# Feed-forward transposes placed six chunks behind their products, relu and square in one VectorE instruction, down projection trailing by six chunks

## The chip, the cores and the metric

The kernel runs on one core of a Trainium2 chip. The metric is the device time of one execution in microseconds. A core has five engines that run side by side, each through its own queue in order: PE (TensorE, matrix products and transposes), DVE (VectorE), ACT (ScalarE), POOL (GpSimd) and SP (SyncE, which only issues loads and stores here). Data comes from HBM into SBUF by DMA, and PE writes its results into PSUM banks.

## The reference

One decoder block on 256 tokens of width 2048, in float32. Only the last part is touched by the change.

```python
proj = x @ w_in                      # conv group and gated linear attention follow
...
mix = concatenate([y_conv, y_gla]) @ w_out
x = layer_norm(DN_ALPHA * x + mix, ln1_g, ln1_b)
ff = square(relu(x @ w_ff_up)) @ w_ff_down      # 2048 -> 8192 -> 2048
x = layer_norm(DN_ALPHA * x + ff, ln2_g, ln2_b)
```

## The kernel before

**Split products.** Every float32 factor is written as a sum of two parts in a shorter format, hi and lo. ACT rounds (`copy`, L108) and DVE subtracts (L109); together that is a *split*. PE then does three matmuls for each pair of tiles (L153 to L155: hi by hi, hi by lo, lo by hi). A weight *chunk* is 256 rows by 512 columns, 512 KB, and takes one load, one split and six matmuls for each half of 128 tokens that it serves. Such six matmuls are called one *product* here.

**Buffers.** Raw chunks lie in 13 buffers (`raw`), split chunks in five (`hl`). A load waits until DVE has freed a raw buffer, and a split waits until PE has freed a split buffer.

**The feed-forward part.** The 8192 hidden columns are eight groups g of 1024. Group 0 (`up_first`) is computed plainly. Groups 1 to 7 (`up`) use a scheme of seven products in place of eight for the 2 x 2 blocks of (tokens, columns): 28 steps s, which are seven phases p of four chunks j. The up chunk of a step is called p_j here (`hl_up_2_3` is phase 2, chunk 3). The phases read these raw tiles: 0: r11; 1: r11 + r12 (DVE, L719), then r11 gets more rows by an accumulating DMA from POOL (L728); 2: r21; 3: the accumulated r11, then accumulated once more; 4: r12 + r22 (DVE, L724, the *third sum*); 5: r22; 6: r11. So four buffers hold r11 over the whole group, four hold r12 from phase 1 to phase 4, and five are left for what streams: r21, r22 and the chunks of the down projection.

Phases end with a combination that gives a 128 x 512 block of the group's output: `end_2` (straight from PSUM bank a), `end_7` (v), `end_3` (x12) and `end_4` (u). Each goes through relu and square, and then `put` transposes it on PE (`pt_h`, L216) and splits it into the pair `hT`, which the down projection reads as its left factor.

**Order on PE.** The products are emitted in the order in which PE is to run them. `lag.after(mm)` is called after every product; it counts down the entries of `lag.soon`, and a transpose whose count is over is ordered behind that product. The main loop at the end runs one up step, adds 4/7 to `owed`, and lets a generator emit one down chunk for each whole unit in `owed`. A down chunk serves both halves of the tokens: two products and two calls of `lag.after`. Names like `dn_512_2` are column block 512, chunk 2. When both chunks and tokens of a column block are done, DVE adds the bank to `y` (L802). A scheduler sets the order on the other engines from the order of the program and its own estimates.

Of the kernel before, what the change touches and what calls it, by code (L numbers as in the profile page):

```python
# [12 lines left out]
AF = mybir.ActivationFunctionType  # L13
ALU = mybir.AluOpType
# [45 lines left out]
def hymba_block(ctx, tc, x, x_t, w_in, conv_w, conv_g, w_gate, gate_b, gla_g, w_out,  # L60
                ln1_g, ln1_b, w_up, w_down, ln2_g, ln2_b, out):
    nc = tc.nc
# [188 lines left out]
    with ExitStack() as p1:  # L251
# [225 lines left out]
        def conv_block(j):  # L477
# [26 lines left out]
            def done_b(t, ps):  # L504
# [8 lines left out]
                for g in range(4):  # L513
                    cols = slice(g * P, (g + 1) * P)
                    nc.vector.scalar_tensor_tensor(y[:, cols], y[:, cols], rstd[:, g:g + 1], cg[:, cols],
                                                   op0=ALU.mult, op1=ALU.mult)
                lag0.soon.append([1 + WAIT_C, lambda: put(y, mixT["conv"], j, t, f"c{j}{t}")])

# [29 lines left out]
    with ExitStack() as p2:  # L548
# [99 lines left out]
        def x1lhs(kt, t):  # L648
            return part(x1T, kt, t)

        def hidden(r, hT, i, t, name, wait):

            nc.vector.tensor_mul(r, r, r)
            lag.soon.append([wait, lambda: put(r, hT, i, t, name)])

        def up_first(hT):

            for i in range(GROUP // NB):
                def done(t, ps, i=i):
                    r = ht.tile([P, NB], F32, tag="relu", name=f"relu_0_{i}_{t}")  # L660
                    nc.scalar.activation(r, ps, AF.Relu)
                    hidden(r, hT, i, t, f"h0_{i}_{t}", 1 + WAIT_H)
                if i == 1:
                    homes[:] = [[(hlp, "hl")], 0]
                    lag.lag = 0
                project(lag, w_up, list(range(KT)), i * NB, NB, x1lhs, done, f"up0_{i}",
                        lags=LAGS if i == 0 else None, before=sums_ahead if i == 1 else None)
# [37 lines left out]
        def up(g, hT):  # L705
# [27 lines left out]
            banks, kept = {}, {}  # L733

            def out(x, i, t, where=None):
                r = x if where is None else where
                nc.scalar.activation(r, x, AF.Relu)
                hidden(r, hT, i, t, f"h{g}_{i}_{t}", 2)

            def end_1():  # L740
                kept["p1"] = tmp("p1")
# [40 lines left out]
            for s, (p, j) in enumerate(steps):  # L782
                _, lhs, bank, then, end = plan[p]
                prepare(s + 1)
                name = f"up{g}_{p}_{j}"
# [78 lines left out]
        downs = iter(())  # L864

        def all_downs():
            for g in range(NG - 1):
                yield from down(g, hTs[g])

        downs, owed = all_downs(), -1.5  # L870
        for g in range(1, NG):
            hTs.append(t8_pair(f"hT_{g}"))
            for _ in up(g, hTs[g]):
# [63 lines left out]
```

## Time and profile before

| | |
|---|---|
| median of 3 runs (lowest to highest) | 1116.71 us (1114.16 to 1119.34) |
| profiled execution: time, span | 1116.4 us, 1114.7 us |
| granted TensorE clock, mean | 0.988 |
| DVE, ACT, POOL busy | 837.2, 598.9, 63.9 us |
| HBM traffic | 222 GB/s over the span |
| up step 1 of group 1 begins, products of group 7 end | about 440, 1048 us |

The span runs from the first to the last instruction. Busy times say how long an engine worked, and the waits say for whom it stood still. An engine that is not the bound may wait at no cost. In rows of a timeline the columns are start, duration, engine, line, operation, tiles and shape, and in brackets the idle time before and who ended it.

### The profile page before, as it was taken

What the parts mean: (1) busy time and instruction counts of PE and PEld (TensorE: products, weight loads), DVE (VectorE), ACT (ScalarE), POOL (GpSimd) and SP (SyncE); (2) the same over time, 40 slices, a digit from 0 to 9 for tenths busy, and PEclk for the clock granted to TensorE, in tenths of its full rate; (3) what the DMA queues carried; (4) which work ended last, traced back from release to release, by engine and by line L of the source; (5) the groups of instructions that cost most, each with busy time, mean ns of one, the idle gap of its engine ahead of it and who ended that gap; (6) DMA issues with size and microseconds to landing.
All of it is one profiled execution on the core that took longest, in us unless ns stands there. A gap on an engine that the chain in (4) does not pass through costs nothing.

```text
span 1114.7 us, 13469 instructions
## 1 busy us (share of the span) xinstructions
PE 1071.6 (96%) x4914; PEld 896.2 (80%) x4914; DVE 837.2 (75%) x958; ACT 598.9 (54%) x695; POOL 63.9 (6%) x74
## 2 busy tenths in 40 slices
PE   9999999999999899999999999999989999989994
PEld 8998888888888778788878877877878877878884
DVE  6555558477655879689789789789879978968867
ACT  6476544436633545556546556556556655645531
POOL 0000000000000110100110110110110110010001
PEclk9999999999999999999999999999999999999998
DMA  9876267676766542997887888788698688688821
GB/s 337 306 254 206 83 209 256 206 225 216 263 225 194 164 159 107 252 258 244 242 228 267 226 228 285 201 239 296 165 252 297 168 251 300 174 232 273 278 63 75
DMA packets 76743, 248.06 MB, mean 223 GB/s; under 512 B 8003, under 2 KB 18259, under 8 KB 76422
## 3 DMA queue, kind: packets, MB, share of 16 engines
q1 hardware_dynamic: 65024, 207.78, 54.7%
q0 software_dynamic: 8064, 29.36, 14.5%
q10 hardware_dynamic: 3590, 10.08, 2.5%
q8 instruction: 38, 0.62, 0.2%
q14 instruction: 27, 0.22, 0.1%
HBM read 244.03 MB, written 3.15 MB: 222 GB/s over the span
## 4 chain that ended last, share of the span: by engine, by line
PE 68%; DVE 14%; DMA 12%; issue 4%; ACT 2%; SPq 0%; DVEq 0%; ACTq 0%
DMA raw_dn<-in_w_ff_down_dram 6%; PE ps_dn L154 6%; PE ps_dn L153 6%; PE ps_dn L155 6%; DMA raw_r<-in_w_ff_up_dram 5%; DVE hl_up L109 5%; DVE hl_dn L109 3%; PE ps_p L155 3%; PE ps_p L153 3%; PE ps_p L154 3%; PE ps_o L155 2%; PE ps_o L154 2%; PE ps_o L153 2%; PE ps_upd L154 2%; PE ps_upd L153 2%
## 5 line engine op out<-in xcount | busy, mean ns | idle before, releaser
L108 ACT CAST hl_up<-raw_r 128x1024 fp32r<-128x1024 f32 x196 | 205.6, 1052 | 107.6 <-PE ps_dn L155 51.5
L109 DVE TENSOR_TENSOR hl_up<-raw_r,hl_up 128x1024 fp32r<-128x1024 f32 x196 | 237.4, 1219 | 30.9 <-ACT hl_up L108 28.4
L108 ACT CAST hl_dn<-raw_dn 128x1024 fp32r<-128x1024 f32 x128 | 134.8, 1053 | 142.8 <-PE ps_dn L155 77.1
L109 DVE TENSOR_TENSOR hl_dn<-raw_dn,hl_dn 128x1024 fp32r<-128x1024 f32 x128 | 156.1, 1220 | 54.4 <-ACT hl_dn L108 53.1
L154 PE MATMUL ps_dn<-hl_dn,hT_hi 128*128 128x512 f32 x496 | 193.5, 390 | 0.5 <-DVE hl_dn L109 0.5
L153 PE MATMUL ps_dn<-hl_dn,hT_hi 128*128 128x512 f32 x496 | 193.3, 390 | 0.0
L155 PE MATMUL ps_dn<-hl_dn,hT_lo 128*128 128x512 f32 x496 | 193.1, 389 | 0.0
L154 PEld LDWEIGHTS ps_dn<-hl_dn,hT_hi 128*128 128x128 f32 x496 | 93.1, 188 | 20.8 <-DVE hl_dn L109 1.3
L153 PEld LDWEIGHTS ps_dn<-hl_dn,hT_hi 128*128 128x128 f32 x496 | 93.1, 188 | 19.8
L155 PEld LDWEIGHTS ps_dn<-hl_dn,hT_lo 128*128 128x128 f32 x496 | 93.1, 188 | 19.4
L728 POOL DMA_DIRECT2D raw_r<-in_w_ff_up_dram x56 | 48.5, 866 | 561.7 <-DVE hl_up L109 530.0
L109 DVE TENSOR_TENSOR hl_p<-raw_p,hl_p 128x824 fp32r<-128x824 f32 (+1 forms) x40 | 40.3, 1016 | 33.4 <-ACT hl_p L108 31.7
L109 DVE TENSOR_TENSOR hl_o<-raw_o,hl_o 128x1024 fp32r<-128x1024 f32 x32 | 38.8, 1222 | 32.9 <-ACT hl_o L108 32.5
L108 ACT CAST hl_o<-raw_o 128x1024 fp32r<-128x1024 f32 x32 | 33.4, 1056 | 45.2 <-PE ps_o L155 31.7
L153 PE MATMUL ps_p<-hl_p,xT_hi 128*128 128x412 f32 (+1 forms) x160 | 56.2, 351 | 0.2 <-ACT xT_hi L108 0.2
L154 PE MATMUL ps_p<-hl_p,xT_hi 128*128 128x412 f32 (+1 forms) x160 | 56.2, 351 | 0.0
L155 PE MATMUL ps_p<-hl_p,xT_lo 128*128 128x412 f32 (+1 forms) x160 | 55.8, 349 | 0.3
L724 DVE TENSOR_TENSOR raw_r<-raw_r,raw_r 128x1024 f32<-128x1024 f32 x28 | 34.2, 1222 | 28.0 <-DMA raw_r<-in_w_ff_up_dram 28.0
L108 ACT CAST hl_p<-raw_p 128x824 fp32r<-128x824 f32 (+1 forms) x40 | 35.1, 885 | 27.1 <-PE ps_p L155 21.4
L154 PE MATMUL ps_upa<-hl_up,x1T_hi 128*128 128x512 f32 x112 | 44.1, 394 | 0.0
L153 PE MATMUL ps_upc<-hl_up,sum_s 128*128 128x512 f32 x112 | 44.1, 394 | 0.0
L153 PE MATMUL ps_upa<-hl_up,x1T_hi 128*128 128x512 f32 x112 | 43.7, 391 | 0.0
(281 smaller groups left out, 2168.2 us busy)
## 6 DMA issues: line engine op xcount, KB each, us to landing
raw_dn<-in_w_ff_down_dram SPq DMA_DIRECT2D x128, 512.0 KB, 5.0
raw_r<-in_w_ff_up_dram SPq DMA_DIRECT2D x112, 512.0 KB, 5.3
raw_r<-in_w_ff_up_dram POOLq DMA_DIRECT2D x56, 512.0 KB, 8.1
raw_o<-in_w_out_dram SPq DMA_DIRECT2D x32, 512.0 KB, 3.5
raw_p<-in_w_in_dram SPq DMA_DIRECT2D x24, 412.0 KB, 5.7
raw_c<-in_w_in_dram SPq DMA_DIRECT2D x16, 512.0 KB, 3.7
raw_u<-in_w_in_dram SPq DMA_DIRECT2D x16, 512.0 KB, 4.3
raw_b<-in_w_in_dram SPq DMA_DIRECT2D x16, 512.0 KB, 4.2
```

The lines of the kernel that those rows point to most:

```text
L108: queued("act", lambda: nc.scalar.copy(hi, src))
L109: queued("dve", lambda: nc.vector.tensor_sub(lo, src, hi.bitcast(F32)))
L153: nc.tensor.matmul(ps[:, :ncol], ah, whi[:, j, cols], start=f, stop=False, skip_group_check=more)
L154: nc.tensor.matmul(ps[:, :ncol], ah, wlo[:, j, cols], start=False, stop=False, skip_group_check=more)
L155: nc.tensor.matmul(ps[:, :ncol], al, whi[:, j, cols], start=False, stop=e, skip_group_check=more)
L724: nc.vector.tensor_add(r12[j], r12[j], r22[j])
L728: return lambda j: nc.gpsimd.dma_start(r11[j], piece(w_up, KH + KC * j, at, NB), accum_op=ALU.add)
```

## The change

Three things change, all in the feed-forward part. The transpose of each output block in groups 1 to 7 stands six calls of `lag.after` behind its product, not two. Blocks that lie in SBUF (v, x12, u) go through relu and square in one DVE instruction, max(x, 0) * x; blocks that come from PSUM (group 0 and `end_2`) get two ACT instructions, relu and then square. The down projection starts 6 chunks behind the up steps, not 1.5.

```diff
+WAIT_UP = 6
+BEHIND = 6
...
-        def hidden(r, hT, i, t, name, wait):
-
-            nc.vector.tensor_mul(r, r, r)
+        def hidden(r, x, hT, i, t, name, wait):
+
+            if r is x:
+                nc.vector.scalar_tensor_tensor(r, x, 0.0, x, op0=ALU.max, op1=ALU.mult)
+            else:
+                nc.scalar.activation(r, x, AF.Relu)
+                nc.scalar.activation(r, r, AF.Square)
             lag.soon.append([wait, lambda: put(r, hT, i, t, name)])
...
                     r = ht.tile([P, NB], F32, tag="relu", name=f"relu_0_{i}_{t}")
-                    nc.scalar.activation(r, ps, AF.Relu)
-                    hidden(r, hT, i, t, f"h0_{i}_{t}", 1 + WAIT_H)
+                    hidden(r, ps, hT, i, t, f"h0_{i}_{t}", 1 + WAIT_H)
...
             def out(x, i, t, where=None):
-                r = x if where is None else where
-                nc.scalar.activation(r, x, AF.Relu)
-                hidden(r, hT, i, t, f"h{g}_{i}_{t}", 2)
+                hidden(x if where is None else where, x, hT, i, t, f"h{g}_{i}_{t}", WAIT_UP)
...
-        downs, owed = all_downs(), -1.5
+        downs, owed = all_downs(), -BEHIND
```

The first place to look at is PE in group 2, around the transpose of the block of `end_2`, whose bank `ps_upa` is done with chunk 2_3. Before (each product is cut to its last matmul):

```order
L155 MATMUL ps_upa_4156<-hl_up_2_3_4392,x1T_lo 128x512
...
L155 MATMUL ps_dn_512_0_4409<-hl_dn_512_0_4406,hT_lo 128x512
...
L155 MATMUL ps_dn_512_1_4416<-hl_dn_512_0_4406,hT_lo 128x512
L216 MATMUL pt_h_0_0_4423<-ident,relu_4401 128x128 x4
L153 MATMUL ps_upb_4434<-hl_up_3_0_4430,sum_q 128x512
```

With the change:

```order
L157 MATMUL ps_upa_4057<-hl_up_2_3_4317,x1T_lo 128x512
...
L157 MATMUL ps_upb_4333<-hl_up_3_0_4329,sum_q 128x512
...
L157 MATMUL ps_dn_0_1_4352<-hl_dn_0_0_4342,hT_lo 128x512
...
L157 MATMUL ps_upb_4333<-hl_up_3_1_4359,sum_q 128x512
...
L157 MATMUL ps_upb_4333<-hl_up_3_2_4369,sum_q 128x512
...
L157 MATMUL ps_dn_0_0_4345<-hl_dn_0_2_4381,hT_lo 128x512
L218 MATMUL pt_h_0_0_4390<-ident,relu_4326 128x128 x4
```

Two products lay between bank and transpose; now six do. Beside phase 3 stands the first column block of the down projection, where the second stood.

The second place is DVE in the same group, from the split of up 2_3 to the split behind the last third sum. Before:

```order
L109 TENSOR_TENSOR hl_dn1_512_0_4406<-raw_dn1_512_0_4404,hl_dn1_512_0_4406 128x1024
L724 TENSOR_TENSOR raw_r12_2_0_4221<-raw_r12_2_0_4221,raw_r22_2_0_4495 128x1024
...
L109 TENSOR_TENSOR hl_dn1_512_2_4453<-raw_dn1_512_2_4451,hl_dn1_512_2_4453 128x1024
L653 TENSOR_TENSOR relu_2_4401<-relu_2_4401 128x512
L109 TENSOR_TENSOR hl_up2_3_2_4468<-raw_r11_2_2_4180,hl_up2_3_2_4468 128x1024
L724 TENSOR_TENSOR raw_r12_2_1_4235<-raw_r12_2_1_4235,raw_r22_2_1_4512 128x1024
L109 TENSOR_TENSOR hl_dn1_512_4_4480<-raw_dn1_512_4_4478,hl_dn1_512_4_4480 128x1024
...
L109 TENSOR_TENSOR hl_up2_4_0_4515<-raw_r12_2_0_4221,hl_up2_4_0_4515 128x1024
L724 TENSOR_TENSOR raw_r12_2_2_4268<-raw_r12_2_2_4268,raw_r22_2_2_4544 128x1024
L724 TENSOR_TENSOR raw_r12_2_3_4281<-raw_r12_2_3_4281,raw_r22_2_3_4556 128x1024
L109 TENSOR_TENSOR hl_dn1_512_6_4527<-raw_dn1_512_6_4525,hl_dn1_512_6_4527 128x1024
```

With the change:

```order
L729 TENSOR_TENSOR raw_r12_2_0_4127<-raw_r12_2_0_4127,raw_r22_2_0_4403 128x1024
L111 TENSOR_TENSOR hl_up2_3_0_4329<-raw_r11_2_0_4050,hl_up2_3_0_4329 128x1024
L111 TENSOR_TENSOR hl_dn1_0_0_4342<-raw_dn1_0_0_4340,hl_dn1_0_0_4342 128x1024
L729 TENSOR_TENSOR raw_r12_2_1_4160<-raw_r12_2_1_4160,raw_r22_2_1_4437 128x1024
...
L111 TENSOR_TENSOR hl_up2_3_2_4369<-raw_r11_2_2_4081,hl_up2_3_2_4369 128x1024
L729 TENSOR_TENSOR raw_r12_2_2_4174<-raw_r12_2_2_4174,raw_r22_2_2_4450 128x1024
L111 TENSOR_TENSOR hl_dn1_0_2_4381<-raw_dn1_0_2_4379,hl_dn1_0_2_4381 128x1024
...
L111 TENSOR_TENSOR hl_up2_4_1_4453<-raw_r12_2_1_4160,hl_up2_4_1_4453 128x1024
L111 TENSOR_TENSOR hT_2_lo_4049<-pt_h2_0_0_4390,hT_2_hi_4048 128x4x128
L729 TENSOR_TENSOR raw_r12_2_3_4206<-raw_r12_2_3_4206,raw_r22_2_3_4481 128x1024
L111 TENSOR_TENSOR hl_dn1_0_6_4464<-raw_dn1_0_6_4462,hl_dn1_0_6_4464 128x1024
```

The square (L653) is gone from between them, and the second and third of the four third sums stand earlier against the chunks of phase 3, the fourth behind the split of `hT`.

The third place is SP's queue where group 1 opens. Before:

```order
L112 DMA raw_r12_1_1_3594<-in_w_ff_up_dram 128x1024
L112 DMA raw_dn0_0_0_3608<-in_w_ff_down_dram 128x1024
L112 DMA raw_r12_1_2_3627<-in_w_ff_up_dram 128x1024
L112 DMA raw_r12_1_3_3640<-in_w_ff_up_dram 128x1024
L112 DMA raw_dn0_0_2_3653<-in_w_ff_down_dram 128x1024
L112 DMA raw_r21_1_0_3670<-in_w_ff_up_dram 128x1024
L112 DMA raw_dn0_0_4_3682<-in_w_ff_down_dram 128x1024
```

With the change:

```order
L114 DMA raw_r12_1_1_3594<-in_w_ff_up_dram 128x1024
L114 DMA raw_r12_1_2_3608<-in_w_ff_up_dram 128x1024
...
L114 DMA raw_r21_1_3_3668<-in_w_ff_up_dram 128x1024
L114 DMA raw_dn0_0_0_3702<-in_w_ff_down_dram 128x1024
L114 DMA raw_dn0_0_2_3741<-in_w_ff_down_dram 128x1024
L114 DMA raw_r22_1_0_3765<-in_w_ff_up_dram 128x1024
L114 DMA raw_dn0_0_4_3782<-in_w_ff_down_dram 128x1024
```

The first down chunk's load stands behind all loads of r12 and r21, and r22_0 follows two loads later. POOL's order is the same in both. From group 2 on, SP's mix of up and down loads is as dense as before, with the down chunks 4.5 later.

## Prediction

> **What bounds the kernel now.** I read the page first, then the list of waits, then the timelines of PE, DVE, ACT and SP around the longest PE waits of the feed-forward part. These are the page's span and busy times:
>
> ```profile
> span 1114.7 us, 13469 instructions
> PE 1071.6 (96%) x4914; PEld 896.2 (80%) x4914; DVE 837.2 (75%) x958; ACT 598.9 (54%) x695; POOL 63.9 (6%) x74
> ```
>
> From the list of waits (us in total, times, longest):
>
> ```profile
> PE pt_h L216 <- DVE relu L653: 17.7, 7, 3.8
> PE pt_h L216 <- DVE v L653: 2.3, 4, 0.7
> DVE raw_r L724 <- DMA raw_r<-in_w_ff_up_dram: 28.0, 17, 3.0
> SPq L112 <- DVE hl_dn L109: 367.1, 118, 15.9
> PE ps_dn L154 <- DVE hl_dn L109: 0.5, 2, 0.3
> ```
>
> PE is the bound: it is idle for 1114.7 - 1071.6 = 43 us in all. 17.7 + 2.3 = 20.0 us of that stand before the feed-forward transposes, which wait for the square (L653) in DVE's queue. Nothing else in the feed-forward part makes PE wait for long yet: the next candidate, a product that waits for DVE's half of a split, costs 0.5 us. But the third and fourth rows say what stands behind: DVE itself waits for r22 (L724), and SP can issue loads only as DVE frees raw buffers.
>
> A wait also costs something after it. These are PE's rows at the five transposes that matter most: the transposes, then the first matmul of the next down chunk, twelve up matmuls later.
>
> ```profile
> 473.87 1.09 PE L216 MATMUL pt_h<-ident,relu 128*128 128x128 f32 x4 [2.57 <-DVE relu L653]
> 478.43 0.39 PE L153 MATMUL ps_dn<-hl_dn,hT_hi 128*128 128x512 f32 x1
> ...
> 561.95 1.03 PE L216 MATMUL pt_h<-ident,relu 128*128 128x128 f32 x4 [2.46 <-DVE relu L653]
> 566.78 0.40 PE L153 MATMUL ps_dn<-hl_dn,hT_hi 128*128 128x512 f32 x1
> ...
> 823.68 0.63 PE L216 MATMUL pt_h<-ident,relu 128*128 128x128 f32 x4 [3.07 <-DVE relu L653]
> 828.50 0.40 PE L153 MATMUL ps_dn<-hl_dn,hT_hi 128*128 128x512 f32 x1
> ...
> 911.40 0.63 PE L216 MATMUL pt_h<-ident,relu 128*128 128x128 f32 x4 [2.33 <-DVE relu L653]
> 914.64 0.39 PE L153 MATMUL ps_dn<-hl_dn,hT_hi 128*128 128x512 f32 x1
> ...
> 1000.36 1.09 PE L216 MATMUL pt_h<-ident,relu 128*128 128x128 f32 x4 [3.82 <-DVE relu L653]
> 1006.10 0.39 PE L153 MATMUL ps_dn<-hl_dn,hT_hi 128*128 128x512 f32 x1
> ```
>
> The same work takes 3.24 us after the wait of 2.33 and 4.56, 4.83, 4.82, 5.74 us after waits of 2.57, 2.46, 3.07, 3.82: PE runs slow for a while after waits of about 2.4 us and more. That is 1.32 + 1.59 + 1.58 + 2.50 = 7.0 us. All that the change could win at the transposes is 20.0 + 7.0 = 27.0 us, 3.9 per group of the seven.
>
> The Trainium skill (TensorE: Matmul & The Clock Gate, Part 1) says that PE's clock falls back after at least one idle window of about 3.4 us. By that only the wait of 3.82 would be slowed, and the win would be at most 22.5 us; the rows show a loss from 2.46 us on, so the trace decides. The sum does not use the page.
>
> **The chain behind the wait.** Rows of the first planned group (g=1): the split of up 2_2 and its product; r22_0's issue, the first third sum; the split of dn 512_4, the issue of r22_3 that follows it, the last third sum, the split of dn 512_6 and its product.
>
> ```profile
> 460.92 1.22 DVE L109 TENSOR_TENSOR hl_up<-raw_r,hl_up 128x1024 fp32r<-128x1024 f32 x1
> 465.70 0.39 PE L153 MATMUL ps_upa<-hl_up,x1T_hi 128*128 128x512 f32 x1
> 467.06 0.39 PE L153 MATMUL ps_upa<-hl_up,x1T_hi 128*128 128x512 f32 x1
> 462.17 0.33 SPq L112 DMA_DIRECT2D raw_r<-in_w_ff_up_dram  x1
> 467.30 1.23 DVE L724 TENSOR_TENSOR raw_r<-raw_r,raw_r 128x1024 f32<-128x1024 f32 x1 [1.30 <-DMA raw_r<-in_w_ff_up_dram]
> 475.92 1.22 DVE L109 TENSOR_TENSOR hl_dn<-raw_dn,hl_dn 128x1024 fp32r<-128x1024 f32 x1
> 477.16 0.33 SPq L112 DMA_DIRECT2D raw_r<-in_w_ff_up_dram  x1
> 484.24 1.23 DVE L724 TENSOR_TENSOR raw_r<-raw_r,raw_r 128x1024 f32<-128x1024 f32 x1 [2.16 <-DMA raw_r<-in_w_ff_up_dram]
> 485.38 1.22 DVE L109 TENSOR_TENSOR hl_dn<-raw_dn,hl_dn 128x1024 fp32r<-128x1024 f32 x1
> 488.18 0.39 PE L154 MATMUL ps_dn<-hl_dn,hT_hi 128*128 128x512 f32 x1
> ```
>
> DVE ends split 2_2 at T = 462.14; SP issues r22_0 at once into the buffer so freed, and it lands 5.1 us later. Nine DVE instructions after that sum, the split of dn 512_4 ends at 477.14 and frees the buffer for r22_3, which lands 7.1 us later. Then the third sum and the split of dn 512_6 end at 486.6 = T + 24.5. PE's product starts at 488.18, only 1.6 us later, although PE had just lost 2.57 + 1.32 = 3.9 us at the transposes. Without that loss PE would come at 484.3 and wait 2.3 us. So part of the old wait is a cover for this chain. PE's step is 467.06 - 465.70 = 1.36 us for an up chunk, twice that for a down chunk.
>
> How early split 2_2 ends before its product (call it s) is 465.92 - 462.14 = 3.8 us here (465.92 is its second matmul, 465.70 + 0.22, the first that reads what DVE writes), and differs between groups; two others, the best and the worst:
>
> ```profile
> 635.11 1.22 DVE L109 TENSOR_TENSOR hl_up<-raw_r,hl_up 128x1024 fp32r<-128x1024 f32 x1
> 641.99 0.39 PE L154 MATMUL ps_upa<-hl_up,x1T_hi 128*128 128x512 f32 x1
> ...
> 987.64 1.22 DVE L109 TENSOR_TENSOR hl_up<-raw_r,hl_up 128x1024 fp32r<-128x1024 f32 x1
> 991.16 0.39 PE L154 MATMUL ps_upa<-hl_up,x1T_hi 128*128 128x512 f32 x1
> ```
>
> That is 5.7 and 2.3 us; I take s = 4.0, the middle of the two ends.
>
> **The change, part by part.** The rows that price it: the square on DVE, the same shape as a scalar_tensor_tensor from SBUF, a Square on ACT; then an accumulating load's time to landing in 446 to 470 us, the first one of group 1, and the first matmul of group 1.
>
> ```profile
> L653 DVE TENSOR_TENSOR relu<-relu 128x512 f32<-128x512 f32 x11 | 7.5, 683 | 0.0
> L693 DVE SCALAR_TENSOR_TENSOR sum_s<-y,y x2: 683/685/687, 402.0 to 424.7; 128x512 f32<-128x512 f32 x2
> L508 ACT ACTIVATE csq<-c 128x512 f32<-128x512 f32 x4 | 2.5, 624 | 3.1 <-DVE c L506 3.1
> raw_r<-in_w_ff_up_dram POOLq DMA_DIRECT2D x3, 512.0 KB, 9.7
> 443.85 1.01 POOL L728 DMA_DIRECT2D raw_r<-in_w_ff_up_dram  x1 [46.39 <-DVE hl_up L109]
> 440.28 0.39 PE L153 MATMUL ps_upa<-hl_up,x1T_hi 128*128 128x512 f32 x1
> ```
>
> Relu and square: 21 outputs (v, x12, u in seven groups) lose a Relu on ACT, and DVE's square becomes one scalar_tensor_tensor of the same 0.68 us. The other 11 (4 of group 0, 7 of end_2) lose DVE's 0.68 us and gain a Square of 0.62 us on ACT. DVE does 7.5 us less over the run, ACT 21 - 11 = 10 instructions less. Nothing of it is on PE's path once the transposes stand later, so its own term is 0, bounded by 0.6 us per group either way.
>
> Transposes: pt_h for end_2 stood two products (2.7 us) behind its bank; now up 3_0, dn 0_0, up 3_1, 3_2 and half of dn 0_2 lie between, 8.2 us. Relu and Square need 1.2 us and stand on ACT. The longest old wait, 3.82, is under the 5.4 us that are added, so these waits go: -27.0 us (bounds -20.0, if PE slows for other reasons, and -27.0).
>
> Down chunks six behind, in groups 2 to 7. PE's work and DVE's are the same in number, but what lies between split 2_2 and the last third sum changes. On PE from 2_2 on: eight up chunks, four down chunks and a transpose (0.37): 8 x 1.36 + 4 x 2.72 + 0.37 = 22.1 us (before 7 x 1.36 + 3 x 2.72 + 0.37 = 18.1). On DVE: r22_0 lands at T + 5.1; third sum 0, splits 3_0 and dn 0_0 end at T + 8.5 (1.14 from start to start: 485.38 - 484.24); that frees r22_2's buffer. Let a load take L. Third sum 2, dn 0_2, 3_3 and dn 0_4 follow, 4 x 1.14: T + 13.1 + L; this frees r22_3's buffer; it lands after L, and third sum 3 and split dn 0_6 take 2.4: T + 15.5 + 2L. PE then waits 15.5 + 2L - 22.1 - s = 2L - 6.6 - 4.0. For L the rows give 5.1 and 7.1; I take the middle, 6.1, as one accumulating load stands before r22_2 and more before r22_3. The wait is 1.6, say 1.5 us, under the length that slows PE. Six groups: +9.0 us. With L = 5.1 it is 0; with 7.1 it is 3.6 and some 2 of slowing, 34 us in all.
>
> Group 1 opens with 13 up chunks alone (before 5). SP issues dn 0_0 behind r12 and r21 there, and r22_0 two loads later. The chunk step k starts on PE at 440.3 + 0.7 + 1.36 k. A split ends 2.3 us (cast and subtraction) after the chunk five before it has left PE, since there are five split buffers: r21_1 is free at 450.1, r22_0 lands at 456.2 with L = 6.1, third sum 0 and dn 0_0 end at 458.5; PE wants it at 458.7. The accumulated r11_0 (443.85 + 9.7 = 453.6) is in time. r22_2 lands at 464.6, dn 0_2 is split at 466.9, PE wants it at 464.1: 2.8 us, with the slowing of 1.3; dn 0_6 0.8 us more. +5 us (bounds 1.5 and 8 with L = 5.1 and 7.1).
>
> The end: 4.5 down chunks more stand alone after the last up chunk. Each is 2.72 us on PE over 1.22 us of DVE, and a load of 5 to 7 us with five buffers or more: 0. POOL's order is unchanged; its accumulating loads are released by the same splits, and are in L. hT: the last reader of the old pair is up step 10's down chunk, ahead of the first transpose at step 14: 0. Banks: the two of the last down pair are freed behind third sum 1, before bank d is wanted: 0.
>
> Sum against the profiled execution (1116.4 us, 0.3 under the median of the runs): 1116.4 - 27.0 + 9.0 + 5.0 = 1103.4 us; for the median the same within 0.3.
>
> **The rivals.** (a) Nothing takes the place of the wait: L = 5.1, groups 2 to 7 at 0, the opening 1.5: 1091 us. For it: r22_0's 5.1; against: r22_3's 7.1 and slack of 1.6 us with the old wait still there. (b) No change: the wait moves whole to the third sums. L = 6.6 gives 2.6 per group, 15.6; the slowing of about 1.4 in half of the groups, 4; the opening 7: 1116 us. For it: DVE's 28.0 us of waits at L724 already. (c) Slower: third sum 2 now stands in front of dn 0_2, where it stood behind up 4_0, so a late load stops DVE sooner. It decides from L = 6.8 on: a wait of 3.0 with slowing of 1.6 in each of six groups is 27.6, the opening 7.5, and the time 1124.5. A load can be as late and later:
>
> ```profile
> 449.68 0.33 SPq L112 DMA_DIRECT2D raw_dn<-in_w_ff_down_dram  x1
> 458.69 1.05 ACT L108 CAST hl_dn<-raw_dn 128x1024 fp32r<-128x1024 f32 x1 [3.98 <-DMA raw_dn<-in_w_ff_down_dram]
> ```
>
> This load took 9.0 us behind group 1's accumulating loads. At the 7.1 of r22_3 it is 5.6 per group, 34, the opening 8: 1131 us. Against it: fewer accumulating loads stand before r22_2 than stood before that one.
>
> **How the numbers follow.** The partial win 0.45, (a) 0.19, (b) 0.20, (c) 0.16. The time is the partial win's, 1103.4; its own range is 1096 to 1110. The whole range reaches to (a)'s 1091 less a little, and past (b): 1090 to 1119, which leaves out (c) and little else. What a measurement can tell from no change is about 0.5%, 5.6 us: faster 0.45 + 0.19 = 0.64, same 0.20, slower 0.16.
>
> **What would show it.** Right: the rows pt_h <- DVE are gone, PE waits at dn 0_2 and dn 0_6 for hl_dn <- DVE by 1 to 2 us per group, L724's wait for DMA grows above 28.0 us. Wrong: no such PE wait (a), or waits over 2.4 us with slow products behind them (b, c); in group 1 a wait outside dn 0_0 to dn 0_6, or any wait in the last six chunks of the down projection behind the up chunks.

## The result, and the profile after

The changed kernel takes 1122.62 us (median of 11 runs, 1118.13 to 1129.25); the kernel before, beside it, 1116.71 us (11 runs, 1114.06 to 1119.34). The ratio is 1.0059, with a 95% interval of 1.0035 to 1.0084: slower by 0.6%, where 1103.4 us were forecast. The profiled execution took 1124.35 us. Its span and busy times:

```profile
span 1122.6 us, 13440 instructions
PE 1076.3 (96%) x4914; PEld 898.6 (80%) x4914; DVE 830.2 (74%) x947; ACT 591.9 (53%) x685; POOL 64.1 (6%) x74
```

The list of waits of the changed kernel (us in total, times, longest); L729 is the third sum, L733 the accumulating load, L110 and L111 the split:

```profile
DVE raw_r L729 <- DMA raw_r<-in_w_ff_up_dram: 56.3, 25, 8.1
ACT hl_dn L110 <- DMA raw_dn<-in_w_ff_down_dram: 43.2, 14, 4.1
PE ps_dn L156 <- DVE hl_dn L111: 23.4, 12, 5.8
```

All waits of PE for the input of a feed-forward transpose are gone. DVE's wait for r22 has doubled (28.0 us before), and PE waits 23.4 us for the splits of down chunks, where it was 0.5. The work has become a little less (DVE 7.0 us, ACT 7.0 us), which helps nobody.

To compare kernels I add up from PE's timeline all waits over 0.25 us after 440 us and what the matmuls right behind each take more than at full speed (0.23 us from start to start). I call this sum the *loss*. It is 20.3 + 8.6 = 28.9 us before and 23.2 + 11.5 = 34.7 us after, good to about 1 us. (Expectations below that speak of 29.5 us for before count one wait of 0.65 us twice.) Of the latter, 9.95 us are at the opening of group 1 (5.85 + 2.48 at dn 0_0, 1.52 + 0.10 at dn 0_6) and 24.8 in groups 2 to 7, 4.1 per group, all at dn 0_2 and dn 0_6.

**The opening.** SP's issues of dn 0_0 and r22_0; the third sum of r22_0 and the split of dn 0_0 on DVE; the product of dn 0_0 on PE:

```profile
450.42 0.33 SPq L114 DMA_DIRECT2D raw_dn<-in_w_ff_down_dram  x1
451.55 0.33 SPq L114 DMA_DIRECT2D raw_r<-in_w_ff_up_dram  x1
...
463.46 1.23 DVE L729 TENSOR_TENSOR raw_r<-raw_r,raw_r 128x1024 f32<-128x1024 f32 x1 [8.11 <-DMA raw_r<-in_w_ff_up_dram]
464.60 1.22 DVE L111 TENSOR_TENSOR hl_dn<-raw_dn,hl_dn 128x1024 fp32r<-128x1024 f32 x1
...
465.87 0.79 PE L156 MATMUL ps_dn<-hl_dn,hT_hi 128*128 128x512 f32 x1 [5.85 <-DVE hl_dn L111]
466.46 0.63 PE L157 MATMUL ps_dn<-hl_dn,hT_lo 128*128 128x512 f32 x1
```

r22_0 took 463.46 - 451.55 = 11.9 us to land. dn 0_0 itself was late as well: ACT waited for it and could round only from 460.17 on, 9.75 us after its issue:

```profile
460.17 1.04 ACT L110 CAST hl_dn<-raw_dn 128x1024 fp32r<-128x1024 f32 x1 [1.10 <-DMA raw_dn<-in_w_ff_down_dram]
```

PE came to dn 0_0 at 460.02. With cast and subtraction the split could have ended at about 462.4 without the third sum, so by this estimate some 2.4 of the 5.85 us are the down chunk's own load and the rest the third sum ahead of its split. What stood beside the two loads is told by the DMA view of 440 to 470 us (bytes and share of the 16 DMA engines by queue; then issues with the median time to landing):

```profile
q0 software_dynamic: 745, 2.72, 51.2%
q1 hardware_dynamic: 720, 2.62, 23.1%
...
raw_r<-in_w_ff_up_dram POOLq DMA_DIRECT2D x7, 512.0 KB, 8.3
raw_dn<-in_w_ff_down_dram SPq DMA_DIRECT2D x2, 512.0 KB, 12.3
```

The accumulating loads (q0) carried about as many bytes as the plain ones (q1) and held the DMA engines for 2.2 times as long.

**A later group, g = 4**, the costliest. In order: splits 2_1 and 2_2 (DVE); issue of r22_0 (SP); split of dn 0_0; issues of r22_1 and r22_2; third sum 2; split of dn 0_4; an accumulating load (POOL) and the issue of r22_3; third sum 3 and the split of dn 0_6; its product.

```profile
712.58 2.59 DVE L111 TENSOR_TENSOR hl_up<-raw_r,hl_up 128x1024 fp32r<-128x1024 f32 x2
715.19 0.33 SPq L114 DMA_DIRECT2D raw_r<-in_w_ff_up_dram  x1
...
723.59 1.22 DVE L111 TENSOR_TENSOR hl_dn<-raw_dn,hl_dn 128x1024 fp32r<-128x1024 f32 x1
...
721.10 4.07 SPq L114 DMA_DIRECT2D raw_r<-in_w_ff_up_dram  x2
...
731.97 1.23 DVE L729 TENSOR_TENSOR raw_r<-raw_r,raw_r 128x1024 f32<-128x1024 f32 x1 [1.73 <-DMA raw_r<-in_w_ff_up_dram]
...
735.38 1.22 DVE L111 TENSOR_TENSOR hl_dn<-raw_dn,hl_dn 128x1024 fp32r<-128x1024 f32 x1
735.91 0.88 POOL L733 DMA_DIRECT2D raw_r<-in_w_ff_up_dram  x1 [4.49 <-DVE hl_up L111]
736.63 0.33 SPq L114 DMA_DIRECT2D raw_r<-in_w_ff_up_dram  x1
...
745.62 1.22 DVE L729 TENSOR_TENSOR raw_r<-raw_r,raw_r 128x1024 f32<-128x1024 f32 x1 [6.15 <-DMA raw_r<-in_w_ff_up_dram]
746.76 1.22 DVE L111 TENSOR_TENSOR hl_dn<-raw_dn,hl_dn 128x1024 fp32r<-128x1024 f32 x1
748.03 0.80 PE L156 MATMUL ps_dn<-hl_dn,hT_hi 128*128 128x512 f32 x1 [3.34 <-DVE hl_dn L111]
```

This is the predicted chain link by link: SP issues r22_2 at 724.84 (0.33 before the end of its row), when the split of dn 0_0 has freed a buffer, and r22_3 at 736.63, when that of dn 0_4 has. Only the loads are slower than assumed: r22_2 takes 7.1 us, r22_3 9.0 us. An accumulating load was issued 0.6 us before the one and 0.7 us before the other.

### The profile page after: what moved, and what is told of

It reads as the page before. It is cut to its first block, busy times and chain, and to the rows that moved or that the text cites. A ratio compares the mean times of both kernels' runs of the same rounds, so it can differ in the third digit from the quotient of the medians.

```text
span 1122.6 us, 13440 instructions
## 1 busy us (share of the span) xinstructions
PE 1076.3 (96%) x4914; PEld 898.6 (80%) x4914; DVE 830.2 (74%) x947; ACT 591.9 (53%) x685; POOL 64.1 (6%) x74
## 3 DMA queue, kind: packets, MB, share of 16 engines
q1 hardware_dynamic: 65024, 207.78, 54.7%
q0 software_dynamic: 8064, 29.36, 14.9%
## 4 chain that ended last, share of the span: by engine, by line
PE 75%; DMA 12%; DVE 9%; issue 2%; ACT 1%; SPq 0%; DVEq 0%
DMA raw_r<-in_w_ff_up_dram 12%; PE ps_dn L156 8%; PE ps_dn L157 7%; PE ps_dn L155 7%; DVE hl_up L111 3%; DVE hl_dn L111 3%; PE ps_p L157 3%; PE ps_p L155 3%; PE ps_p L156 3%; PE ps_o L156 2%; PE ps_o L155 2%; PE ps_o L157 2%; PE ps_upc L155 2%; PE ps_upc L157 2%; PE ps_upc L156 2%
## 5 line engine op out<-in xcount | busy, mean ns | idle before, releaser
L110 ACT CAST hl_up<-raw_r 128x1024 fp32r<-128x1024 f32 x196 | 205.8, 1053 | 125.7 <-PE ps_dn L157 55.4
L111 DVE TENSOR_TENSOR hl_up<-raw_r,hl_up 128x1024 fp32r<-128x1024 f32 x196 | 237.2, 1219 | 14.6 <-ACT hl_up L110 11.1
L156 PE MATMUL ps_dn<-hl_dn,hT_hi 128*128 128x512 f32 x496 | 198.5, 400 | 23.4 <-DVE hl_dn L111 23.4
L110 ACT CAST hl_dn<-raw_dn 128x1024 fp32r<-128x1024 f32 x128 | 134.8, 1053 | 154.0 <-PE ps_dn L157 83.1
L155 PE MATMUL ps_dn<-hl_dn,hT_hi 128*128 128x512 f32 x496 | 197.6, 398 | 0.0
L111 DVE TENSOR_TENSOR hl_dn<-raw_dn,hl_dn 128x1024 fp32r<-128x1024 f32 x128 | 156.0, 1220 | 55.5 <-ACT hl_dn L110 54.0
L157 PE MATMUL ps_dn<-hl_dn,hT_lo 128*128 128x512 f32 x496 | 197.0, 397 | 0.0
L156 PEld LDWEIGHTS ps_dn<-hl_dn,hT_hi 128*128 128x128 f32 x496 | 95.1, 192 | 48.4 <-DVE hl_dn L111 29.2
L155 PEld LDWEIGHTS ps_dn<-hl_dn,hT_hi 128*128 128x128 f32 x496 | 94.7, 191 | 19.7
L733 POOL DMA_DIRECT2D raw_r<-in_w_ff_up_dram x56 | 48.6, 868 | 555.0 <-DVE hl_up L111 539.7
L729 DVE TENSOR_TENSOR raw_r<-raw_r,raw_r 128x1024 f32<-128x1024 f32 x28 | 34.3, 1225 | 56.4 <-DMA raw_r<-in_w_ff_up_dram 56.3
L111 DVE TENSOR_TENSOR hl_p<-raw_p,hl_p 128x824 fp32r<-128x824 f32 (+1 forms) x40 | 40.3, 1017 | 33.4 <-ACT hl_p L110 31.7
L111 DVE TENSOR_TENSOR hl_o<-raw_o,hl_o 128x1024 fp32r<-128x1024 f32 x32 | 38.8, 1223 | 32.8 <-ACT hl_o L110 32.5
L110 ACT CAST hl_o<-raw_o 128x1024 fp32r<-128x1024 f32 x32 | 33.5, 1056 | 45.2 <-PE ps_o L157 38.5
L110 ACT CAST hl_p<-raw_p 128x824 fp32r<-128x824 f32 (+1 forms) x40 | 35.1, 884 | 26.9 <-PE ps_p L157 21.3
L155 PE MATMUL ps_upa<-hl_up,x1T_hi 128*128 128x512 f32 x112 | 44.4, 396 | 0.0
L157 PE MATMUL ps_upa<-hl_up,x1T_lo 128*128 128x512 f32 x112 | 43.7, 390 | 0.0
```

Of the source, the lines that this page charges most:

```text
L110: queued("act", lambda: nc.scalar.copy(hi, src))
L111: queued("dve", lambda: nc.vector.tensor_sub(lo, src, hi.bitcast(F32)))
L155: nc.tensor.matmul(ps[:, :ncol], ah, whi[:, j, cols], start=f, stop=False, skip_group_check=more)
L156: nc.tensor.matmul(ps[:, :ncol], ah, wlo[:, j, cols], start=False, stop=False, skip_group_check=more)
L157: nc.tensor.matmul(ps[:, :ncol], al, whi[:, j, cols], start=False, stop=e, skip_group_check=more)
L729: nc.vector.tensor_add(r12[j], r12[j], r22[j])
```

## The experiments

Ratios are to the kernel before, run beside on the same chip, with 95% intervals; the loss is that of the profiled execution. "Late" means six calls for the transposes, "early" two; "merged" is the new relu and square; "lag" is by how many chunks the down projection trails.

| kernel | transposes, relu and square, lag, raw buffers | median us | ratio | loss us |
|---|---|---|---|---|
| before | early, old, 1.5, 13 | 1116.7 | 1 | 28.9 |
| after | late, merged, 6, 13 | 1122.6 | 1.0059 (1.0035 to 1.0084) | 34.7 |
| e1 | late, merged, 1.5, 13 | 1109.0 | 0.9926 (0.9905 to 0.9947) | 18.0 |
| e2 | early, old, 6, 13 | 1136.2 | 1.0162 (1.0137 to 1.0187) | 53.5 |
| e3 | early, merged, 1.5, 13 | 1132.6 | 1.0125 (1.0089 to 1.0162) | 44.1 |
| e4 | after without accumulating loads | 1086.3 | one run | 0 |
| e5 | before without accumulating loads | 1087.2 | one run | 0 |
| e6 | late, old, 1.5, 13 | 1126.7 | 1.0063 (1.0039 to 1.0087) | 37.7 |
| e7 | late, merged, 1.5 growing to 6 in group 2, 13 | 1118.3 | 0.9994 (0.9971 to 1.0016) | 28.3 |
| e8 | late, merged, 6, 14 | 1095.3 | 0.9785 (0.9759 to 0.9810) | 5.6 |
| e9 | late, merged, 1.5, 14 | 1087.4 | 0.9726 (0.9711 to 0.9740) | 0 |
| e10 | early, old, 1.5, 14 | 1111.0 | 0.9936 (0.9919 to 0.9953) | 21.2 |
| e11 | after with the smaller pools of e8 | 1120.2 | 1.0029 (1.0011 to 1.0047) | 35.2 |
| e12 | late, merged, 6, 12 | 1121.1 | 1.0036 (1.0020 to 1.0052) | 29.4 |
| e13 | late, old, 1.5, 14 | 1086.7 | 0.9717 (0.9702 to 0.9731) | 0 |
| e14 | early, merged, 1.5, 14 | 1089.4 | 0.9743 (0.9725 to 0.9762) | 1.3 |
| e15 | after, third sums 2 and 3 behind splits | 1099.2 | 0.9843 (0.9800 to 0.9886) | 14.2 |
| e16 | e1, third sums 2 and 3 behind splits | 1095.4 | 0.9810 (0.9758 to 0.9863) | 5.9 |

The profiled time less the loss is between 1086 and 1092 us in all eighteen (before 1116.4 - 28.9 = 1087.5; after 1124.35 - 34.7 = 1089.7; e2 1143.3 - 53.5 = 1089.8; e13 1086.6). Within these 6 us nothing but the loss tells the kernels apart, so what has to be explained in each is where PE waits.

**e1: the change without its lag.**

```diff
-BEHIND = 6
+BEHIND = 1.5
```

> Transposes six products late and the new relu and square, but the down projection 1.5 chunks behind as before. Theory (the loss sits in the chain of third sums and r22 loads, made longer by the down projection's new place): the waits at the transposes go (29.5 us with the slow matmuls behind them, in the trace of before), the opening of group 1 is as before, and PE waits only 1 to 2 us per group at the split behind the last third sum, since 24 us of chain stand against 18.1 us of products and a lead of 4 to 6 us: about 1099 us, ratio 0.984. Rival 1 (the late transposes hold up DVE, which waits for PE before the splits of hT): as slow as the change, about 1122. Rival 2 (Square on ACT is the cost): also slower than before, with waits for ACT.

Measured 1109.0 us. The direction holds: the lag is the part that harms. The size does not, since 18.0 us of loss stay, in short waits at other splits. Its waits:

```profile
ACT hl_dn L110 <- DMA raw_dn<-in_w_ff_down_dram: 64.0, 14, 7.9
DVE raw_r L729 <- DMA raw_r<-in_w_ff_up_dram: 41.1, 21, 4.3
PE ps_dn L156 <- DVE hl_dn L111: 7.8, 11, 1.0
PE ps_upb L156 <- DVE hl_up L111: 7.2, 7, 1.9
```

**e2: the lag alone.**

```diff
-        downs, owed = all_downs(), -1.5
+        downs, owed = all_downs(), -6
```

> Only the down projection six chunks behind; transposes two products late and relu and square as before. Theory: the opening of group 1 loses some 10 us as in the change (a wait of 5.9 and one of 1.5 there), and the waits at the transposes stay, so slower than before by 5 to 15 us: about 1126, ratio 1.008. Rival 1 (late transposes are the cost): no slower than before, 1117 or below, with no wait at dn 0_0 in group 1.

Measured 1136.2 us, worse than expected. The waits of the transposes stay as a whole (24.0 us), and the opening adds one of 6.55 us at dn 0_0 with 1.58 behind it.

**e3: the merged instruction alone.**

```diff
-WAIT_UP = 6
-BEHIND = 6
+WAIT_UP = 2
+BEHIND = 1.5
```

> Only the new relu and square; transposes two products late, the down projection 1.5 chunks behind. Theory: the block of end_2 goes through ACT alone, which is done 1.3 us after the bank, and PE comes to its transpose 2.7 us after it, so the 17.7 us of waits for the square in DVE's queue go without any move of the transposes; PE then waits 1 to 2 us per group behind the last third sum: about 1100 us, ratio 0.985, the same as with late transposes within 5 us. Rival 2 (Square on ACT costs): slower than before, waits of PE for ACT. If the transposes' place matters by itself: 1110 or more, with waits left at pt_h.

Measured 1132.6 us: a miss of 33 us. The waits for the relu of `end_2` are gone, as they should be with the square on ACT, but others are there:

```profile
ACT hl_dn L110 <- DMA raw_dn<-in_w_ff_down_dram: 89.3, 20, 9.5
PE pt_h L218 <- DVE v L656: 12.2, 7, 2.1
PE ps_upb L156 <- DVE hl_up L111: 12.2, 7, 2.6
```

ACT waits up to 9.5 us for down chunks to land, the splits behind them are late, and the transpose of v waits in every group, 2.1 us in five of the seven (2.3 us in all before).

**e4 and e5: without the accumulating loads.** In both kernels the load is left out:

```diff
-                return lambda j: nc.gpsimd.dma_start(r11[j], piece(w_up, KH + KC * j, at, NB), accum_op=ALU.add)
+                return None
```

> The change with the 56 accumulating loads left out (phases 3 and 6 then use r11 as it stands, so part of the up projection is not computed). Theory: the r22 loads and the first down chunks are late because accumulating loads share the DMA engines with them in the same few us; without them a load lands in 4 to 5 us, PE's waits for hl_dn (23.4 us and 11.5 us of slow matmuls) go, and the time is 1122.6 - 34.9 = about 1088. Rival (the order on DVE alone makes the wait, loads are late only because buffers are freed late): the waits stay above 12 us, 1105 or more.

> The kernel before without the accumulating loads of phases 1 and 3 (56 of 512 KB), so the phases 3 and 6 of each group read other numbers; the amount of work on PE, ACT and DVE stays. Theory (the old waits before the transposes come from the same transfers: DVE stands at the third sum for r22, and the square behind it is late): the waits pt_h <- DVE relu fall from 17.7 us to under 4, and the 29.5 us of waits and slow products after 440 us go nearly whole: about 1089 us. Rival (the square is simply placed too late in DVE's order, whatever the transfers do): the waits stay above 10 us, and the time is 1100 us or more.

Measured 1086.3 and 1087.2 us, each with no wait of PE over 0.25 us after 440 us. DVE's wait at the third sum in e4, then in e5:

```profile
DVE raw_r L729 <- DMA raw_r<-in_w_ff_up_dram: 10.8, 18, 1.3
```

```profile
DVE raw_r L724 <- DMA raw_r<-in_w_ff_up_dram: 3.4, 7, 0.7
```

DVE's order of splits and third sums is in e4 that of the changed kernel and in e5 that of the kernel before, in all seven groups, so the order alone makes no wait; in e4 r22_3 lands after 3.4 to 3.6 us. So the old waits at the transposes and the new ones at the down chunks need the same thing, the burst of transfers with the 56 accumulating loads in it. Without these, neither of the two kernels loses anything to its place of the transposes or its lag. The loads go with their bytes, 12% of the traffic; whether the same bytes by plain loads would do the harm was not tried.

**e6: late transposes, old relu and square.**

```diff
-            if r is x:
-                nc.vector.scalar_tensor_tensor(r, x, 0.0, x, op0=ALU.max, op1=ALU.mult)
-            else:
-                nc.scalar.activation(r, x, AF.Relu)
-                nc.scalar.activation(r, r, AF.Square)
+            nc.scalar.activation(r, x, AF.Relu)
+            nc.vector.tensor_mul(r, r, r)
...
-BEHIND = 6
+BEHIND = 1.5
```

> Only the transposes are moved (six calls in place of two); relu and square are the old two instructions, and the down projection trails by 1.5. Theory (the whole gain of the earlier run at 1.5 with both, 1109.0 us, is the lateness; the merged instruction is worth nothing by itself): 1109 within 3 us. Rival 1 (the merged instruction does harm by the order that DVE gets, as the run with it alone at 1132.6 us says): faster than 1106 us. Rival 2 (the merged instruction earns its share, 10 instructions less on ACT and 11 less on DVE): 1112 us or more.

Measured 1126.7 us: rival 2's direction, but by far more than its saved instructions could earn. No transpose waits; one down chunk per group does:

```profile
PE ps_dn L156 <- DVE hl_dn L111: 24.8, 7, 4.8
```

Against e1 the merged instruction is worth 1.4% here, and in e3 it costs 1.2%. Whether that is the instruction or the place at which DVE then stands for a load was left to e13 and e14. With 13 buffers each of the three parts alone (e2, e3, e6) is slower than before.

**e7: the lag without its opening.**

```diff
-        downs, owed = all_downs(), -BEHIND
+        downs, owed = all_downs(), -1.5
...
-                owed += 4 / 7
+                owed += 4 / 7 - (BEHIND - 1.5) / 28 * (g == 2)
```

> The changed kernel, but the down projection starts 1.5 chunks behind and falls back to 6 behind evenly over the 28 steps of group 2. Waits and slow products after 440 us in the changed kernel: 9.95 us at the first down chunk of group 1 and 24.8 us in groups 2 to 7; with 1.5 throughout 2.3 and 15.7. Theory (both the opening and the steady place of the chunks cost): group 1 as at 1.5, groups 3 to 7 as in the changed kernel: 2.3 + 2 + 23.1 = 27.4 against 18.0, so 1109.0 + 9.4 = 1118 us. Rival 1 (the opening is all the harm, the steady lag none): 1109 to 1111. Rival 2 (the opening is none of it): 1122 or more.

Measured 1118.3 us, as the theory had it, though its parts were off and made up for each other: the loss is 3.4 us in group 1, 5.5 in group 2 and 19.4 in groups 3 to 7, where 2.3, 2 and 23.1 were expected. The changed kernel has 9.95, 1.7 and 23.0. The opening and the steady lag both cost.

**e8 and e11: one raw buffer more, and its control.** The room comes from two small pools.

```diff
-RAWS = 13
+RAWS = 14
...
-        ht = p2.enter_context(tc.tile_pool(name="ht", bufs=2))
+        ht = p2.enter_context(tc.tile_pool(name="ht", bufs=1))
...
-        sm2 = p2.enter_context(tc.tile_pool(name="sm2", bufs=2))
+        sm2 = p2.enter_context(tc.tile_pool(name="sm2", bufs=1))
```

> The changed kernel with 14 raw buffers in place of 13 (room from one tile each of the relu and the small statistics tiles). Theory (the waits come from the chain of loads through the five streaming buffers: each load can go out only when DVE has freed a buffer): one buffer more lets each r22 go out one chunk earlier, 1.4 to 2.7 us, the waits at dn 0_2 and dn 0_6 (15.8 + 8.9 us in groups 2 to 7) fall to under a third, the opening to some 6 us: 1098 to 1105 us. Rival (the transfers themselves are the limit while the accumulating loads run, and an earlier issue only queues longer): L729's wait for DMA stays near 56 us, and the time within 5 us of 1122.6.

> Control: the changed kernel with 13 raw buffers but with the one relu tile and the one set of small statistics tiles of the runs with 14. Theory: the smaller pools by themselves are worth nothing, 1120 to 1125 us, as the changed kernel. Rival (they reorder DVE, and part of the gain of the runs with 14 is theirs): under 1115 us.

e8 takes 1095.3 us, a little better than the theory's best; the smaller pools alone (e11, 13 buffers) change nothing, 1120.2 us. The waits of e8, then group 4's issues of r22_1 and r22_2 and their third sum 2:

```profile
DVE raw_r L729 <- DMA raw_r<-in_w_ff_up_dram: 41.1, 14, 5.2
PE ps_upb L156 <- DVE hl_up L111: 2.9, 1, 2.9
PE ps_dn L156 <- DVE hl_dn L111: 0.3, 1, 0.3
```

```profile
707.15 3.87 SPq L114 DMA_DIRECT2D raw_r<-in_w_ff_up_dram  x2
...
712.85 1.22 DVE L111 TENSOR_TENSOR hl_dn<-raw_dn,hl_dn 128x1024 fp32r<-128x1024 f32 x1
...
717.45 1.22 DVE L729 TENSOR_TENSOR raw_r<-raw_r,raw_r 128x1024 f32<-128x1024 f32 x1
```

r22_2 goes out at 710.69 (the end of its row less 0.33), ahead of the split of dn 0_0 at 712.85, behind which it stood with 13 buffers, and the third sum finds it landed. DVE still waits 41.1 us for DMA in all; but no longer in front of a split that PE is about to need. The scheduler has also given DVE another order: an up chunk's split and that of `hT` stand between third sum 3 and the split of dn 0_6 in groups 2 to 7. So e8 alone does not separate the earlier load from the order; e15 does.

**e9, e10, e12: the buffers in other company.** e9 is e1 and e10 the kernel before, each with the edit of e8; e12 is the changed kernel with

```diff
-RAWS = 13
+RAWS = 12
```

> 14 raw buffers as in the earlier run with the changed kernel (1095.3 us), and the down projection 1.5 behind, as in the run at 1.5 (1109.0 us with 13 buffers and 18.0 us of waits and slow products). Theory (the lag costs only because buffers are short): without waits of note both lags come to the same, so 1091 to 1096 us, ratio near 0.978. Rival (the lag of 1.5 is better in itself, by some 13 us as with 13 buffers): 1085 us or less.

> The kernel before with 14 raw buffers (one tile each of the relu and the small statistics tiles gives the room), nothing else. Theory (the old waits before the transposes, 29.5 us with the slow products, are DVE standing at the third sums for a load that a buffer held back): they fall to under 8 us, 1090 to 1096 us, ratio near 0.978, so the three parts of the change are worth nothing once the buffer is there. Rival (late transposes are worth something of their own: the square stands behind splits in DVE's queue even with all loads in time): 10 us of waits at pt_h or more stay, 1100 us or more.

> The changed kernel with 12 raw buffers, four of them for what streams. Theory (each buffer fewer holds every r22 back by about one more chunk of PE, 1.4 to 2.7 us, at each of two to four points of a group, and slow products follow): from 34.7 us of waits and slow products to 70 or more, 1155 to 1190 us. Rival (with 13 the transfers, not the buffers, were already the limit): under 1135 us.

e9: 1087.4 us and no wait left, the lowest that a whole kernel with the merged form gave. The lag of 6 costs 1095.3 - 1087.4 = 7.9 us even with 14 buffers, between theory and rival. e10: 1111.0 us, and here the rival has the time and the waits right:

```profile
DVE raw_r L724 <- DMA raw_r<-in_w_ff_up_dram: 21.9, 8, 4.4
PE pt_h L216 <- DVE relu L653: 14.8, 7, 2.5
```

With the buffer the old place of the transposes still costs 21.2 us. The rival's reason, that the square stands behind splits even with all loads in time, is not shown, since the loads are not in time: DVE still waits for r22_0 in every group, 2.5 to 4.4 us at third sum 0, and from that sum to the square it works without a break (723.33 to 730.21 in group 4). In each group this wait is longer than PE's for the square (1.7 to 2.5 us). In e5, where r22_0 costs DVE 0.7 us at most, the square stands behind the same sum and one split less, and PE waits for no square. So the early transposes are more exposed to a late load, and that is what they cost here. e12 contradicts the theory: one buffer fewer costs nothing (1.0036, against 1.0059 with 13). Its waits are spread:

```profile
DVE raw_r L729 <- DMA raw_r<-in_w_ff_up_dram: 32.7, 20, 3.5
PE ps_dn L156 <- DVE hl_dn L111: 11.9, 12, 2.5
```

DVE's order is another one there. Rows of group 3 in e12: the split of dn 0_6 and behind it the last third sum:

```profile
657.34 1.23 DVE L111 TENSOR_TENSOR hl_dn<-raw_dn,hl_dn 128x1024 fp32r<-128x1024 f32 x1 [2.12 <-ACT hl_dn L110]
...
659.08 1.21 DVE L729 TENSOR_TENSOR raw_r<-raw_r,raw_r 128x1024 f32<-128x1024 f32 x1
```

With 13 buffers the sum stands ahead of that split (745.62 and 746.76 in group 4 above), and a late r22_3 holds it up. So the count of buffers is not all; e15 and e16 take up the order.

**e13 and e14: relu and square with loads in time.** e6 and e3, each with the edit of e8.

> Late transposes, the old two instructions for relu and square, the down projection 1.5 behind, 14 raw buffers. Theory (the merged instruction mattered only through where DVE stood for late loads): 1087 within 3 us, as with the merged one. Rival (DVE's longer work counts by itself): 1095 us or more.

> The merged instruction alone with early transposes, the down projection 1.5 behind, 14 raw buffers. The order of DVE with 13 buffers had one split between the subtraction that makes v and its square, and the transpose of v waited 2.1 us in six of seven groups (12.2 us). Theory (the splits' waits of 12 us at up 3_0 go with the buffer, the waits of the transposes for a square that stands too late in DVE's queue stay): 1100 to 1112 us, with 12 us or more of waits at pt_h. Rival (all of it was the loads): under 1095 us.

e13: 1086.7 us without a wait, the fastest of the kernels that do all of the work; behind late transposes the merged instruction is worth nothing. e14: 1089.4 us, and the theory's 12 us of waits at the transposes are not there:

```profile
DVE raw_r L729 <- DMA raw_r<-in_w_ff_up_dram: 22.7, 9, 4.0
PE pt_h L218 <- DVE v L656: 0.5, 1, 0.5
```

So e3's 12.2 us in front of v's transpose, too, went with the shortage of buffers. With 14 buffers either part alone, late transposes or the square of `end_2` on ACT, takes 22 to 24 us out of the kernel before (1111.0), and the second adds nothing. The swings of 1.2 to 1.4% that the instruction made with 13 buffers are not its own cost.

**e15 and e16: the order of the third sums alone.** The loads and the 13 buffers stay as they are; the third sums 2 and 3 of each group are ordered on DVE behind the split of the latest down chunk. e15 is the changed kernel with

```diff
-            yield kts[i:i + KC], *parts_of(raw, ncol, f"{name}_{i}")
+            parts = parts_of(raw, ncol, f"{name}_{i}")
+            split_of[name[:2]] = nc.cur_bb.bb.instructions[-1]
...
-                nc.vector.tensor_add(r12[j], r12[j], r22[j])
+                with tc.issue_after(split_of["dn"]) if j >= 2 else nullcontext():
+                    nc.vector.tensor_add(r12[j], r12[j], r22[j])
```

and e16 has BEHIND = 1.5 besides.

> The changed kernel with 13 raw buffers, but the third sums 2 and 3 of each group ordered on DVE behind the split of the latest down chunk (dn 0_4 and dn 0_6), not ahead of it. Theory (a late r22 costs PE only because the third sum holds up the split of a down chunk behind it): the waits at dn 0_2 and dn 0_6 of groups 2 to 7, 24.8 us with the slow products, fall to under 10, the opening's 10 us stay: 1104 to 1110 us. Rival (the load is late for the up chunk that needs the sum as well, and the wait only moves to up 4_2 and 4_3): 1117 us or more, with waits for hl_up <- DVE in phase 4.

> The same order of the third sums at a lag of 1.5 (late transposes, merged instruction, 13 raw buffers), to be held against 1109.0 us and a loss of 18.0 us with the sums ahead. Theory: the waits at dn 512_6 (0.8 to 1.0 us per group) go, those at up 3_0 (1.0 to 1.9 us) stay: 1100 to 1105 us. Rival (the waits move to up 4_2 and 4_3): 1108 us or more.

e15 takes 1099.2 us, 0.9843 of before; e16 1095.4 us, where e1 took 1109.0. Both are better than the theory's best. The loss of e15 is 8.8 us at the opening, which the edit leaves as it was, and 5.4 in groups 2 to 7, where the changed kernel has 24.8. Waits of e15:

```profile
DVE raw_r L734 <- DMA raw_r<-in_w_ff_up_dram: 21.5, 19, 8.5
PE ps_dn L160 <- DVE hl_dn L113: 6.9, 3, 6.2
PE ps_upd L160 <- DVE hl_up L113: 2.2, 4, 0.8
```

The waits do not move to the up chunks of phase 4 to any size (2.2 us). The loads did not get faster: in groups 2 to 7 of e15 r22_3 took 8.8 to 10.5 us, against 7.1 to 9.0 in the changed kernel. The late load costs PE in groups 2 to 7 because the sum that waits for it stands, in DVE's queue, ahead of a split that PE needs sooner.

## Why the prediction was wrong

**What held.** The transposes' waits went, as forecast: -27.0 us forecast, 28.9 us by the count used here. In groups 2 to 7 the new waits are where they were put, at dn 0_2 and 0_6, with hl_dn <- DVE as their releaser; L729's wait grew above 28.0 us; the 4.5 chunks at the end wait for nothing.

**The step that failed is the load time L.** Both positive terms were worked out with one L = 6.1, the middle of 5.1 (r22_0) and 7.1 (r22_3). The chain of groups 2 to 7 goes through r22_2 and r22_3, and in the changed kernel these took 5.9 to 7.1 us (mean 6.4) and 7.1 to 9.0 us (mean 7.9): 14.3 us together, where 2L = 12.2 was put. The trace of before could have told it, since r22_3 took 7.05 to 7.7 us there in every group, and only r22_0 less (4.6 to 6.1). The prediction also quoted a load of 9.0 us beside group 1's accumulating loads, and set it aside.

With each group's own two loads and nothing else changed, the prediction's sum gives waits of 2.6, 3.4, 5.5, 4.1, 2.4 and 4.0 us in groups 2 to 7; the trace has 1.6, 2.7, 4.3, 3.0, 1.5 and 2.8, lower by 0.7 to 1.2 in each. Group 4 in full: split 2_2 ends at T = 715.17; the split of dn 0_6 ends at 747.98, T + 32.8, where 15.5 + 7.1 + 9.0 = 31.6 and r22_0's own 6.1 in place of 5.1 make T + 32.6. PE comes at T + 22.1 + s, with s = 5.9 here (4.0 assumed, so the error of s was in the forecast's favour): the wait is 32.8 - 28.0 = 4.8; the trace has 0.95 at dn 0_2 and 3.34 at dn 0_6 with 0.2 of slow matmuls between.

**A second term was put at nothing by a limit that does not exist.** The wait of 1.5 us per group was held to be "under the length that slows PE". In groups 2 to 7 the waits are 15.8 us and the slow matmuls behind them 8.9 us, and two of these stretches (1.7 us each) follow waits of 1.97 and 2.29 us; the last section says what decides.

The two terms then read: groups 2 to 7, +9.0 forecast, +24.8 measured (4.1 per group, not 1.5); the opening, +5.0 forecast, +9.95 measured. The opening's wait is also at another place than forecast: dn 0_0, put at no wait, has 5.85 us, since its own load and r22_0's took 9.75 and 11.9 us; dn 0_2, put at 2.8, has none, since r22_2 took 3.4. 1116.4 - 28.9 + 34.7 = 1122.2 against the profiled 1124.35.

This is rival (c): it was to decide from L = 6.8, with 1124.5 us. That this is so near is in part luck, since its terms are 27.6 and 7.5 where 24.8 and 9.95 were measured. Its mechanism, third sum 2 ahead of dn 0_2, is the smaller part: of the 15.8 us of waits 2.35 are at dn 0_2 and 13.5 at dn 0_6, behind third sum 3. Its chance of 0.16 rested on "fewer accumulating loads stand before r22_2"; but in group 4 r22_2 was issued 0.6 us and r22_3 0.7 us behind one.

**The cover that the change took away** was named in the prediction (the old wait covers the chain of loads), and its price was too low. The old wait at the transposes gave the loads 1.7 to 3.8 us in each group. With it gone, PE and DVE run into the same loads earlier: DVE's wait at the last third sum was 1.1 to 3.0 us before and is 4.3 to 6.2 us in groups 2 to 7, with the split of dn 0_6 right behind it. Three runs show the chain, each by another link: take the accumulating loads away (e4, loss 0), give r22_2 a buffer one split earlier, with another order of DVE (e8, 5.6), or let the sum alone stand behind the split (e15, 14.2, of which 8.8 at the opening).

**The term of the merged instruction**, 0 within 0.6 us per group, was right as a cost (e9 against e13) and wrong as a bound: with loads short it moves the time by 15 to 18 us either way (e1 against e6, e3 against before), and with a buffer more not at all or by 2% for the better. Which row of DVE's order makes e3 and e6 slow was not tried one by one.

## What to carry to other kernels

A wait that you remove may be the time in which another chain catches up: before counting it as a gain, run that chain with the load times of its own transfers, and with the slowest that the trace shows near them, not with the middle of two different ones. On an engine that works in order, an instruction that waits for a transfer belongs behind whatever the bound engine needs sooner; by the ratios, moving two sums per group took 2.1% off the changed kernel (e15) and one streaming buffer more 2.7% (e8), while the change itself cost 0.6%. Price the parts of a change with the shared shortage taken away: then either late transposes or the merged instruction gave 2%, the second of them nothing more, and the lag cost 0.7%.

## What the runs showed of the hardware

**Accumulating loads are dear.** 56 of them (29.36 MB) held 14.9% of the DMA engines' time in the changed kernel, the plain loads and all else of the SP queue (207.78 MB) 54.7%: 0.51% per MB against 0.26%. Plain loads issued near them landed after as much as 7 to 12 us (r22_3 of groups 2 to 7, r22_0 of group 1), though not all did (r22_2 of group 1 took 3.4). After 440 us the median of r's plain loads was 5.5 us with them and 4.1 us without (e4).

**PE's slow stretch lasts one or two fixed steps, and the length of a wait alone does not set it off.** After a wait of 1.97 us in the changed kernel the steps from matmul to matmul go from 0.23 to 0.43 us between 839.65 and 842.64; the wait, the first full slow row and the last:

```profile
838.03 0.50 PE L156 MATMUL ps_dn<-hl_dn,hT_hi 128*128 128x512 f32 x1 [1.97 <-DVE hl_dn L111]
...
839.65 0.63 PE L156 MATMUL ps_dn<-hl_dn,hT_hi 128*128 128x512 f32 x1
...
842.64 0.48 PE L157 MATMUL ps_upd<-hl_up,sum_s 128*128 128x512 f32 x1
```

In e7 nothing slows behind a wait of 3.10 us:

```profile
568.37 0.50 PE L156 MATMUL ps_dn<-hl_dn,hT_hi 128*128 128x512 f32 x1 [3.10 <-DVE hl_dn L111]
...
572.39 0.39 PE L155 MATMUL ps_upd<-hl_up,sum_s 128*128 128x512 f32 x1
```

The prediction took 2.4 us as the length from which PE slows; there is none such. The granted clock in the traces shows what decides. In the changed kernel it is at 0.5 from 463.93, 658.49, 747.24, 839.40 and 1013.48 us, each time for 3.41 or 6.83 us, and these starts lie 57, 83, 110 and 161 whole steps of 3.41 us behind the first. So time is cut into steps of 3.41 us that do not care when the matmuls come. The wait of 1.97 us lies whole in the step that ends at 839.40. The wait of 3.10 us is cut by the border at 566.5 of e7's own grid into 1.25 and 1.84 us. In the ten traces with waits and a slow stretch by which to place the grid, every full-speed step in which PE was idle for 1.90 us or more (waits over 0.2 us added up) was followed by a step at half clock, and of those with 1.1 to 1.87 us only two, both in e12; a wait counts by what falls into one step, and over half of a step is about the limit. One slow step costs 1.7 us, two some 2.3 to 3.

The Trainium skill (TensorE: Matmul & The Clock Gate, Part 1) speaks of a free-running window of about 3.4 us. The stretch's length and the fixed grid agree with it; that a whole idle window is needed for the clock to fall does not, since 1.97 us sufficed.
